# Half pieces of expert weights split three ahead in all sixteen experts of a hybrid decoder block

## The chip, the core and the metric

The kernel runs on one core of a Trainium2 chip. The metric is the device time of one execution in microseconds; where several executions were timed, their median. The engines go by their names in the profile: PE is TensorE (PEld its weight loads), ACT ScalarE, DVE VectorE, POOL GpSimd, SP the engine that here only issues loads and stores.

## The reference

A block over 512 tokens of width 1024: a norm, a pooling mixer and a gated linear recurrence merged by gates, an output projection with a residual, a second norm, and then the part that the change is about, a mixture of 16 experts. Each token goes to two experts of one group. Cut to that part:

```
def hier_moe(h, rg_w, rg_b, re_w, re_b, e_gate, e_up, e_down):
    ...
    for e in range(N_EXP):                      # 16; e_gate, e_up: 1024x512, e_down: 512x1024
        he = jax.nn.silu(xt @ e_gate[e]) * (xt @ e_up[e])
        y = y + comb[:, e:e + 1] * (he @ e_down[e])
```

After it comes a residual and a last norm with a gain. All of it is float32.

## The kernel before

**The stream of weights.** All weights are one list of 124 chunks of 1 MB (512 x 512 numbers for the experts), in the order in which they are used. A chunk is loaded by SP into a raw tile (load_raw, L138, the issue at L143), with at most three loads in flight. Then it is split in two half pieces (split, L150): ScalarE casts a half to float32r, the high part (L151), and VectorE subtracts that from the raw half, the low part (L152). Raw chunks, split half pieces and the transposed rows xt of an expert are tiles of 8 KB per partition in one pool of twenty (b8). weights (L159) is called each time a product is about to read half piece h of chunk c; it first writes out the splits of all half pieces up to 2*c + h + ahead that haven't been written yet, and then the loads.

```
def weights(c, ahead, raw_ahead, h=1):
    while nxt["split"] <= min(2 * c + h + ahead, 2 * len(chunks) - 1):
```

So ahead says how many half pieces beyond the one in use stand in the queues of ScalarE and VectorE by the time its matmuls are written. Each engine works through its queue in order.

**An expert.** Its rows (128 slots) are gathered by GpSimd into xg, transposed by TensorE and split as well (next_x; L718, L504 and L505), and multiplied by the weights as high x high, high x low and low x high (tok_mm, lines L726, L727, L728): six matmuls for a half piece, of which the first needs ScalarE's cast and the second VectorE's subtraction. The order of the chunks is gate of expert e (2 chunks), down of e - 1 (2), up of e (2). The loop at the end writes: first half of gate(e); the hidden state of e - 1 transposed and split (h_parts: L739, then L504 and L505 into ht); second half of gate(e); down(e - 1) in two halves, each evacuated and scaled by ScalarE (L774) and both scattered by GpSimd into x_acc (L743); the next expert's x; up(e), and then the product of the hidden state (L732 on ScalarE, L733 on VectorE). For the last expert the second half of down(14) comes after up(15). Behind that scatter SP reads x_acc back (L879), and the last norm follows.

**What sets how far ahead.** exp_w is the only caller of weights in the experts; its three constants stand before it: three half pieces ahead for chunks below the first gate chunk of expert 12, one from there on, and loads 14 chunks ahead.

```
SPLIT_AHEAD, LATE_AHEAD, RAW_AHEAD = 3, 1, 14
LATE = 12
...
return lambda h: weights(c, SPLIT_AHEAD if c < c_g[LATE][0] else LATE_AHEAD, RAW_AHEAD, h)[h]
```

A scheduler orders the written instructions of each engine by their dependences and by the order of writing, so a few matmuls and casts stand a little beside the written order.

Of the kernel before, what the change touches and what calls it, by code (L numbers as in the profile page):

```python
# [17 lines left out]
P = 128  # L18
S = 512
D = 1024  # L20
KD = D // P
# [15 lines left out]
def tile_hybrid_block(  # L37
# [19 lines left out]
    def b8(shape, dtype, name):  # L57
        return sb.tile(shape, dtype, tag="b8", name=name, bufs=20)

    def s4(shape, dtype, name):  # L60
        return sb.tile(shape, dtype, tag="s4", name=name, bufs=6)

    def s2(shape, dtype, name):
        return sb.tile(shape, dtype, tag="s2", name=name, bufs=5)

    def bank(name):
        return psum.tile([P, 512], F32, tag="ps", name=name)

    def tiny(shape, dtype, name, bufs=2):
        return sb.tile(shape, dtype, tag=name.split("_")[0] + "_t", name=name, bufs=bufs)  # L70

    class Feat:
        """[P, KD, S] in two tiles."""

        def __init__(self, dtype, name):
            self.t = [b8([P, KD // 2, S], dtype, f"{name}{i}") for i in range(2)]
# [15 lines left out]
    tbl = tc.dram_tile([S * NE, 1], I32, name="slot_ids")  # L92
    tblw = tc.dram_tile([S * NE, 1], F32, name="slot_w")

# [1 line left out]
    chunks = []  # L96

    def add(w, r0, rows, c0, n):
# [17 lines left out]
    c_g, c_u, c_d = {}, {}, {}  # L116
# [16 lines left out]
    raws, pairs, loads = {}, {}, {}  # L133
# [4 lines left out]
    def load_raw(upto, after=None):  # L138
        while nxt["raw"] <= min(upto, len(chunks) - 1):
            j = nxt["raw"]  # L140
            ap, kk, n = chunks[j]
            raws[j] = b8([P, kk, n], F32, f"raw{j}")
            loads[j] = SP.dma_start(raws[j], ap).ins  # L143
            if j - IN_FLIGHT in loads:
                tc.add_manual_dep(loads[j], loads[j - IN_FLIGHT].name, SYNC, reason="loads in flight")
            if after is not None:
                tc.add_manual_dep(loads[j], after.name, SYNC, reason="loads yield to it")
            nxt["raw"] += 1
# [5 lines left out]
    def split_half(r, nm):  # L154
        w = b8([P, 2] + list(r.shape[1:]), F32R, f"w{nm}")
        split(r, w[:, 0], w[:, 1])
        return w

    def weights(c, ahead, raw_ahead, h=1):  # L159
        while nxt["split"] <= min(2 * c + h + ahead, 2 * len(chunks) - 1):  # L160
            i, half = divmod(nxt["split"], 2)
            load_raw(i)
            kh = chunks[i][1] // 2
            pairs.setdefault(i, []).append(split_half(raws[i][:, half * kh:(half + 1) * kh], f"{i}_{half}"))
            if half == 1:
                raws.pop(i)
            nxt["split"] += 1
        load_raw((nxt["split"] - 1) // 2 + raw_ahead)
        return pairs[c]

# [1 line left out]
    x_rows = [s4([P, D], F32, f"x_rows{t}") for t in range(NT)]  # L172
    for t in range(NT):
        SP.dma_start(x_rows[t], xr[t * P:(t + 1) * P, :])
# [3 lines left out]
        SP.dma_start(raws[0][:, 4 * h:4 * h + 4], ap0[:, 4 * h:4 * h + 4])  # L178
    nxt["raw"] = 1

# [1 line left out]
    ident = const.tile([P, P], F32, name="ident")  # L182
    make_identity(nc, ident)
    mhalf = const.tile([P, 1], F32, name="mhalf")
# [21 lines left out]
    g1, lam, cb, br, bi, psc, g2f = (par[n] for n in ("g1", "lam", "cb", "br", "bi", "psc", "g2f"))  # L206
    cw = par["cw"].rearrange("p (j c) -> p j c", j=4)

# [1 line left out]
    def rstd_of(src, name):  # L210
        sq = s2([P, D], BF16, f"sq_{name}")
        ssum = tiny([P, 1], F32, f"ssum_{name}", 4)
        ACT.activation(sq, src, AF.Square, accum_out=ssum)
        ms = tiny([P, 1], F32, f"ms_{name}", 4)
        DVE.tensor_scalar(ms, ssum, 1.0 / D, EPS, op0=ALU.mult, op1=ALU.add)
        rs = tiny([P, 1], F32, f"rs_{name}", 4)
        POOL.tensor_tensor(rs, ms, mhalf, op=ALU.pow)
        return rs
# [31 lines left out]
            mm3(ps, w[:, 0], w[:, 1], hi[k], lo[k], k == 0, k == kk - 1)  # L250
        return ps

# [1 line left out]
    sp8 = const.tile([P, KD], F32, name="sp8")  # L254
    nsp8 = const.tile([P, KD], F32, name="nsp8")

    def softplus():
        def small(name):
            return tiny([P, KD], F32, name, 1)

        nlam, mab, ee, den, ss, s2_, acc = (small(n) for n in
                                            ("nlam", "mab", "ee", "den", "ssr", "ssq", "sacc"))
        DVE.tensor_scalar(nlam, lam, -1.0, None, op0=ALU.mult)
        DVE.tensor_tensor(mab, lam, nlam, op=ALU.min)
        ACT.activation(ee, mab, AF.Exp)
        DVE.tensor_scalar(den, ee, 2.0, None, op0=ALU.add)
        DVE.reciprocal(den, den)
        DVE.tensor_tensor(ss, ee, den, op=ALU.mult)
        DVE.tensor_tensor(s2_, ss, ss, op=ALU.mult)
        DVE.tensor_scalar(acc, s2_, 1.0 / 19.0, 1.0 / 17.0, op0=ALU.mult, op1=ALU.add)  # L270
        for k in (15, 13, 11, 9, 7, 5, 3, 1):
            DVE.tensor_tensor(acc, acc, s2_, op=ALU.mult)
            DVE.tensor_scalar(acc, acc, 1.0 / k, None, op0=ALU.add)
        DVE.tensor_tensor(acc, acc, ss, op=ALU.mult)
        DVE.tensor_scalar(nlam, nlam, 0.0, None, op0=ALU.max)
        DVE.scalar_tensor_tensor(acc, acc, 2.0, nlam, op0=ALU.mult, op1=ALU.add)
        DVE.tensor_scalar(sp8, acc, 8.0, None, op0=ALU.mult)
        DVE.tensor_scalar(nsp8, acc, -8.0, None, op0=ALU.mult)

# [1 line left out]
    ra, ix, uu = Lazy(F32, "ra"), Lazy(F32, "ix"), Lazy(F32, "uu")  # L281
    bd = []

# [45 lines left out]
            lru_gates(*pend.pop(0))  # L329
        pend.append(lru_conv(c, ps))  # L330

# [1 line left out]
    icnt = const.tile([P, PAD], F32, name="icnt")  # L333
    for j in range(PAD):
        POOL.memset(icnt[:, j:j + 1], 1.0 / (j + 1))
# [70 lines left out]
                ACT.copy(yh[cc], uu[cc])  # L406
                DVE.tensor_tensor(yl[cc], uu[cc], yh[cc].bitcast(F32), op=ALU.subtract)

# [1 line left out]
    m = Lazy(F32, "m")  # L410
    for j in range(KD):
        wp = weights(c_ga[j // 2], 4, 2)
# [13 lines left out]
        ps = feat_block(wp, (j % 2) * P, KD, xh, xl, f"zgb{j}")  # L426
        ACT.activation(sgb[j], ps, AF.Sigmoid)

# [1 line left out]
    NR = 2 * NG + NE  # L430
    rw = s2([P, KD, NG + NE], F32, "rw")
    POOL.dma_start(rw[:, :, :NG], router_group_w[0].rearrange("(k p) n -> p k n", p=P))
# [51 lines left out]
    rows = const.tile([P, NE], I32, name="rows")  # L484
# [11 lines left out]
            ACT.copy(mt[i][:, 0, j, :], mj)  # L496
            DVE.tensor_tensor(mt[i][:, 1, j, :], mj, mt[i][:, 0, j, :].bitcast(F32), op=ALU.subtract)

# [1 line left out]
    x2s, h2s, xts, xpart, xg = {}, {}, {}, [], []  # L500

    def evac4(tp, hi, lo):
# [4 lines left out]
    def gather(idx, dst, n=S):  # L507
        return POOL.indirect_dma_start(  # L508
            out=dst, out_offset=None, in_=h2d[:n, :],
            in_offset=bass.IndirectOffsetOnAxis(ap=idx, axis=0),  # L510
            bounds_check=n - 1, oob_is_err=False).ins
# [149 lines left out]
    for t in range(NT):  # L661
# [4 lines left out]
        for n in range(2):  # L666
            po = bank(f"po{t}_{n}")
            for kh in range(2):
                w = weights(c_wo[n][kh], 2 if n + kh < 2 else 0, RA[2 * t + n])
                for kk in range(4):  # L670
# [6 lines left out]
                    if kk % 2 == 1:  # L677
# [3 lines left out]
                        if step == 5 and t == NT - 1:  # L681
                            xg.append(s4([P, D], F32, "xg0"))
                            POOL.memset(xg[0], 0.0)
                            first = gather(rows0, xg[0], (NT - 1) * P)
# [59 lines left out]
            out=xd, out_offset=bass.IndirectOffsetOnAxis(ap=idx, axis=0),  # L744
            in_=src, in_offset=None, bounds_check=S - 1, oob_is_err=False, compute_op=ALU.add)

    SPLIT_AHEAD, LATE_AHEAD, RAW_AHEAD = 3, 1, 14
    LATE = 12

    def exp_w(lst, i):  # L750
        c = lst[i]
        return lambda h: weights(c, SPLIT_AHEAD if c < c_g[LATE][0] else LATE_AHEAD, RAW_AHEAD, h)[h]


    def next_x(e):
# [5 lines left out]
    def up(e):  # L761
        pu = bank(f"pu{e}")
        for i in range(2):
            tok_mm(pu, xts[e], 4 * i, exp_w(c_u[e], i), i == 0, i == 1)
            if e + i == 0:
                next_x(1)
        return pu

    def down(e, ht):
        yt = s4([P, D], F32, f"y{e}")  # L770
        for n in range(2):
            py = bank(f"py{e}_{n}")
            tok_mm(py, ht, 0, exp_w(c_d[e], n), True, True)
            ACT.activation(yt[:, n * 512:(n + 1) * 512], py, AF.Copy, scale=wslot[:, e:e + 1])  # L774
            yield
        scatter_add(rows[:, e:e + 1], yt)

    def gate_half(e, pg, i):
        tok_mm(pg, xts[e], 4 * i, exp_w(c_g[e], i), i == 0, i == 1)

# [1 line left out]
    cn = bank("cn")  # L782
    PE.matmul(cn[:, :NE], ones, acum, start=True, stop=True)
    nmf = const.tile([P, 1], F32, name="nmf")
# [27 lines left out]
    back = s2([P, S], F32R, "back")  # L812
# [3 lines left out]
    for i in range(2):  # L816
        weights(c_d[L][i], 0, 0)

# [1 line left out]
    n_max = nc.values_load(nmi[0:1, 0:1], min_val=0, max_val=S)  # L820
    with tc.If(n_max > P):
        emp = s2([P, S * NE // P], I32, "emp")
# [50 lines left out]
                    ACT.activation(og[:, n * 512:(n + 1) * 512], ps, AF.Copy, scale=wsl)  # L873
                scatter_add(sl, og)

# [1 line left out]
    xb = [b8([P, 2, D], F32, f"xb{i}") for i in range(2)]  # L877
    for t in range(NT):
        SP.dma_start(xb[t // 2][:, t % 2, :], xd[t * P:(t + 1) * P, :])  # L879
# [31 lines left out]
    for t, rs in enumerate(frs):  # L911
        for n in range(2):
            c = slice(n * 512, (n + 1) * 512)
# [37 lines left out]
```

## Time and profile before

| what | us |
|---|---|
| median of 3 runs | 697.93 |
| lowest and highest run | 696.56, 698.88 |
| span of the profiled execution | 695.7 |
| TensorE busy in it | 650.9 |
| VectorE busy | 502.5 |
| ScalarE busy | 431.4 |
| GpSimd busy | 79.6 |

The profile is of one execution; its times count from the first instruction. A timeline row has a start, a duration, the engine and line, what is written from what, and in brackets how long the engine sat idle before it and what it waited for. A busy TensorE is not TensorE at its peak: matmuls overlap, so the step from one start to the next tells more than one duration. [...] The experts begin at about 370 us of the span, and the last four take from about 585 to 665 us.

### The profile page before, as it was taken

What the parts mean: (1) busy time and instruction counts of PE and PEld (TensorE: products, weight loads), DVE (VectorE), ACT (ScalarE), POOL (GpSimd) and SP (SyncE); (2) the same over time, 40 slices, a digit from 0 to 9 for tenths busy, and PEclk for the clock granted to TensorE, in tenths of its full rate; (3) what the DMA queues carried; (4) which work ended last, traced back from release to release, by engine and by line L of the source; (5) the groups of instructions that cost most, each with busy time, mean ns of one, the idle gap of its engine ahead of it and who ended that gap; (6) DMA issues with size and microseconds to landing.
All of it is one profiled execution on the core that took longest, in us unless ns stands there. A gap on an engine that the chain in (4) does not pass through costs nothing. (4 is left out here: it accounts for less than half of the span.)

```text
span 695.7 us, 8405 instructions
## 1 busy us (share of the span) xinstructions
PE 650.9 (94%) x3044; PEld 526.8 (76%) x3044; DVE 502.5 (72%) x792; ACT 431.4 (62%) x579; POOL 79.6 (11%) x101
## 2 busy tenths in 40 slices
PE   5999999999999999999959999999999999999970
PEld 4888888788888888887747787777777777777850
DVE  6886699952322227556687898898899888887946
ACT  6599957752213225141244888888888888777913
POOL 3000000000100000000131111111111111101013
PEclk9999999999999999999988999999999999999996
DMA  7920323213217113696584999999999999999134
GB/s 215 345 79 20 127 81 118 95 62 122 65 62 241 53 69 121 235 389 236 198 310 134 334 333 342 341 351 338 331 337 336 361 336 342 335 339 365 53 98 161
DMA packets 88053, 153.23 MB, mean 220 GB/s; under 512 B 7250, under 2 KB 29894, under 8 KB 88009
## 3 DMA queue, kind: packets, MB, share of 16 engines
q1 hardware_dynamic: 81736, 138.98, 57.5%
q0 software_dynamic: 5824, 12.64, 6.8%
q10 hardware_dynamic: 448, 1.05, 0.4%
q8 instruction: 24, 0.39, 0.2%
q14 instruction: 21, 0.16, 0.1%
HBM read 146.67 MB, written 14.16 MB: 231 GB/s over the span
## 5 line engine op out<-in xcount | busy, mean ns | idle before, releaser
L152 DVE TENSOR_TENSOR w<-raw,w 128x1024 fp32r<-128x1024 f32 x248 | 293.6, 1220 | 69.7 <-ACT w L151 67.6
L151 ACT CAST w<-raw 128x1024 fp32r<-128x1024 f32 x248 | 249.7, 1051 | 59.4 <-DVE w L152 14.1
L727 PE MATMUL pu<-w,xt 128*128 128x512 f32 x128 | 51.9, 406 | 2.3 <-DVE w L152 2.3
L726 PE MATMUL pu<-w,xt 128*128 128x512 f32 x128 | 52.2, 408 | 1.8 <-ACT w L151 1.8
L726 PE MATMUL pg<-w,xt 128*128 128x512 f32 x128 | 52.8, 412 | 1.1
L727 PE MATMUL py<-w,ht 128*128 128x512 f32 x128 | 51.6, 403 | 0.0
L728 PE MATMUL py<-w,ht 128*128 128x512 f32 x128 | 50.7, 396 | 0.6 <-DVE ht L505 0.6
L728 PE MATMUL pg<-w,xt 128*128 128x512 f32 x128 | 50.4, 394 | 0.5 <-DVE xt L505 0.5
L728 PE MATMUL pu<-w,xt 128*128 128x512 f32 x128 | 50.7, 396 | 0.0
L727 PE MATMUL pg<-w,xt 128*128 128x512 f32 x128 | 50.3, 393 | 0.3 <-DVE w L152 0.3
L508 POOL DMA_INDIRECT xg<-h_rows,rows x16 | 26.9, 1679 | 197.6 <-PE xtp L718 177.8
L726 PE MATMUL py<-w,ht 128*128 128x512 f32 x128 | 48.8, 395 | 0.8 <-ACT ht L504 0.8
L743 POOL DMA_INDIRECT x_acc<-y,rows x15 | 24.6, 1639 | 62.9 <-ACT y L774 36.4
L727 PEld LDWEIGHTS pu<-w,xt 128*128 128x128 f32 x128 | 24.5, 191 | 8.8 <-DVE w L152 3.2
L726 PEld LDWEIGHTS pg<-w,xt 128*128 128x128 f32 x128 | 24.1, 188 | 9.4 <-ACT w L151 5.3
L726 PEld LDWEIGHTS pu<-w,xt 128*128 128x128 f32 x128 | 24.3, 190 | 7.7 <-ACT w L151 3.1
L726 PEld LDWEIGHTS py<-w,ht 128*128 128x128 f32 x128 | 24.5, 191 | 6.1 <-ACT ht L504 1.0
L505 DVE TENSOR_TENSOR xt<-xtp,xt 128x512 fp32r<-128x512 f32 x30 | 19.4, 686 | 13.4 <-ACT xt L504 13.4
L727 PEld LDWEIGHTS pg<-w,xt 128*128 128x128 f32 x128 | 24.1, 188 | 6.2 <-DVE w L152 0.7
L728 PEld LDWEIGHTS py<-w,ht 128*128 128x128 f32 x128 | 24.4, 191 | 5.7 <-DVE ht L505 1.0
L728 PEld LDWEIGHTS pg<-w,xt 128*128 128x128 f32 x128 | 24.0, 188 | 5.8 <-DVE xt L505 1.1
L728 PEld LDWEIGHTS pu<-w,xt 128*128 128x128 f32 x128 | 24.5, 191 | 4.8
(292 smaller groups left out, 1414.6 us busy)
## 6 DMA issues: line engine op xcount, KB each, us to landing
raw<-in_exp_w_gate_dram SPq DMA_DIRECT2D x32, 1024.0 KB, 8.0
raw<-in_exp_w_up_dram SPq DMA_DIRECT2D x32, 1024.0 KB, 7.9
raw<-in_exp_w_down_dram SPq DMA_DIRECT2D x32, 1024.0 KB, 10.7
raw<-in_w_in_dram SPq DMA_DIRECT2D x17, 1024.0 KB, 7.7
raw<-in_proj_b_dram SPq DMA_DIRECT2D x4, 1024.0 KB, 9.3
raw<-in_w_out_dram SPq DMA_DIRECT2D x4, 1024.0 KB
x_rows<-in_x_dram SPq DMA_DIRECT2D x4, 512.0 KB
xrow<-in_x_dram SPq DMA_DIRECT2D x4, 512.0 KB
```

What stands on the lines that cost most here:

```text
L151: ACT.copy(hi, r)
L152: DVE.tensor_tensor(lo, r, hi.bitcast(F32), op=ALU.subtract)
L505: DVE.tensor_tensor(lo, tv, hi.bitcast(F32), op=ALU.subtract)
L508: return POOL.indirect_dma_start(out=dst, out_offset=None, in_=h2d[:n, :], in_offset=bass.IndirectOffsetOnAxis(ap=idx, axis=0), bounds_che ...
L726: PE.matmul(ps, hi, w[:, 0, k % 2, :], start=first and k == 0, stop=False)
L727: PE.matmul(ps, hi, w[:, 1, k % 2, :], start=False, stop=False)
L728: PE.matmul(ps, lo, w[:, 0, k % 2, :], start=False, stop=last and k == 3)
L743: POOL.indirect_dma_start(out=xd, out_offset=bass.IndirectOffsetOnAxis(ap=idx, axis=0), in_=src, in_offset=None, bounds_check=S - 1, oob_i ...
```

## The change

From expert 12 on the splits are written three half pieces ahead, as for the first twelve, instead of one. The rest of the diff takes comments out, which moves no instruction; the lines behind L747 are one less in the changed kernel.

```
-    SPLIT_AHEAD, LATE_AHEAD, RAW_AHEAD = 3, 1, 14
-    LATE = 12
+    SPLIT_AHEAD, RAW_AHEAD = 3, 14
 
     def exp_w(lst, i):
         c = lst[i]
-        return lambda h: weights(c, SPLIT_AHEAD if c < c_g[LATE][0] else LATE_AHEAD, RAW_AHEAD, h)[h]
+        return lambda h: weights(c, SPLIT_AHEAD, RAW_AHEAD, h)[h]
```

The first place is ScalarE's queue around the start of up(12). raw_4690 and raw_4718 are the two chunks of up(12), raw_4740 the first of gate(13); w_0 and w_1 are the half pieces of a chunk; y is the result of down(11), xt the rows of expert 13. Before:

```order
L774 ACTIVATE y_5036<-py_0_5037,wslot 128x512
L151 CAST w_0_5069<-raw_4690 128x1024
L504 CAST xt_5084<-xtp_0_5085 128x512
L774 ACTIVATE y_5036<-py_1_5059,wslot 128x512
L504 CAST xt_5084<-xtp_1_5092 128x512
L151 CAST w_1_5103<-raw_4690 128x1024
L151 CAST w_0_5112<-raw_4718 128x1024
L151 CAST w_1_5123<-raw_4718 128x1024
```

In the changed kernel:

```order
L773 ACTIVATE y_5044<-py_0_5045,wslot 128x512
L151 CAST w_1_5068<-raw_4690 128x1024
L151 CAST w_0_5077<-raw_4718 128x1024
L773 ACTIVATE y_5044<-py_1_5067,wslot 128x512
L504 CAST xt_5092<-xtp_0_5093 128x512
L504 CAST xt_5092<-xtp_1_5100 128x512
L151 CAST w_1_5111<-raw_4718 128x1024
L151 CAST w_0_5120<-raw_4740 128x1024
```

One cast more stands ahead of the first half of y and two more ahead of the second, and up(12) has three of its four half pieces cast before xt where it had one.

The second place is VectorE's queue after up(13), between the product of the hidden state (silu) and the low part of its transpose (ht, L505). Before:

```order
L733 TENSOR_TENSOR silu_5297<-silu_5297,pu_5258 128x512
L152 TENSOR_TENSOR w_0_5310<-raw_4921,w_0_5310 128x1024
L152 TENSOR_TENSOR w_1_5327<-raw_4921,w_1_5327 128x1024
L152 TENSOR_TENSOR w_0_5336<-raw_4964,w_0_5336 128x1024
L505 TENSOR_TENSOR ht_5319<-htp_5320,ht_5319 128x512
```

In the changed kernel:

```order
L733 TENSOR_TENSOR silu_5303<-silu_5303,pu_5266 128x512
L152 TENSOR_TENSOR w_1_5307<-raw_4921,w_1_5307 128x1024
L152 TENSOR_TENSOR w_0_5316<-raw_4964,w_0_5316 128x1024
L505 TENSOR_TENSOR ht_5325<-htp_5326,ht_5325 128x512
L152 TENSOR_TENSOR w_1_5333<-raw_4964,w_1_5333 128x1024
```

The half pieces between the two are one fewer; the one that left stands ahead of silu.

The third place is the end of ScalarE's queue in the experts: the two halves of y of expert 14, between them what is left to cast of its last down chunk (raw_5231 and raw_5271 before, raw_5217 and raw_5239 in the changed kernel are the two chunks of down(15)). Before:

```order
L774 ACTIVATE y_5489<-py_0_5490,wslot 128x512
L151 CAST w_0_5568<-raw_5231 128x1024
L151 CAST w_1_5581<-raw_5231 128x1024
L151 CAST w_0_5584<-raw_5271 128x1024
L151 CAST w_1_5587<-raw_5271 128x1024
L774 ACTIVATE y_5489<-py_1_5558,wslot 128x512
```

In the changed kernel:

```order
L773 ACTIVATE y_5495<-py_0_5496,wslot 128x512
L732 ACTIVATE silu_5553<-pg_5450 128x512
L151 CAST w_1_5565<-raw_5217 128x1024
L151 CAST w_0_5574<-raw_5239 128x1024
L151 CAST w_1_5587<-raw_5239 128x1024
L773 ACTIVATE y_5495<-py_1_5564,wslot 128x512
```

Three casts stand between the two halves of y where four stood, and the activation of the hidden state of expert 15 (L732) has come between.

## Rows read from the trace of the kernel before

**Rows 1.** The page's first part: busy us (share of the span) xinstructions.
```profile
PE 650.9 (94%) x3044; PEld 526.8 (76%) x3044; DVE 502.5 (72%) x792; ACT 431.4 (62%) x579; POOL 79.6 (11%) x101
```

**Rows 2.** By stage: length, busy PE, PEld, DVE, ACT, POOL (xinstructions), clock, DMA, GB/s.
```profile
580.26:598.50 18.24, 18.13 (x88) 14.56 (x86) 15.89 (x17) 14.13 (x18) 3.45 (x2) 1.00 1.02 354
598.50:618.11 19.61, 18.27 (x87) 14.60 (x86) 16.39 (x16) 15.33 (x18) 2.62 (x2) 1.00 0.99 340
618.11:639.52 21.41, 19.89 (x87) 15.80 (x86) 16.55 (x16) 15.43 (x20) 1.56 (x1) 0.92 1.01 353
639.52:655.52 16.00, 14.81 (x67) 11.67 (x66) 15.25 (x16) 15.82 (x20) 2.15 (x2) 1.00 0.47 150
655.52:663.46 7.94, 7.94 (x37) 6.57 (x35) 7.94 (x10) 4.89 (x6) 0.00 (x0) 1.00 0.01 3
```

**Rows 3.** TensorE's timeline: start us, us, engine, line, operation, [idle before, releaser].
```profile
592.70 0.39 PE L728 MATMUL py<-w,ht 128*128 128x512 f32 x1
...
600.72 0.51 PE L726 MATMUL pu<-w,xt 128*128 128x512 f32 x1 [0.59 <-ACT w L151]
601.98 0.50 PE L727 MATMUL pu<-w,xt 128*128 128x512 f32 x1 [0.75 <-DVE w L152]
...
620.50 0.49 PE L726 MATMUL pu<-w,xt 128*128 128x512 f32 x1 [0.75 <-ACT w L151]
621.76 0.50 PE L727 MATMUL pu<-w,xt 128*128 128x512 f32 x1 [0.77 <-DVE w L152]
...
640.77 0.40 PE L728 MATMUL pu<-w,xt 128*128 128x512 f32 x1
641.58 0.49 PE L726 MATMUL pu<-w,xt 128*128 128x512 f32 x1 [0.42 <-ACT w L151]
642.84 0.50 PE L727 MATMUL pu<-w,xt 128*128 128x512 f32 x1 [0.77 <-DVE w L152]
643.18 0.40 PE L728 MATMUL pu<-w,xt 128*128 128x512 f32 x1
...
660.96 0.39 PE L726 MATMUL py<-w,ht 128*128 128x512 f32 x1
...
663.46 0.39 PE L728 MATMUL py<-w,ht 128*128 128x512 f32 x1
```

**Rows 4.** ScalarE's timeline, the same columns; x2, x4: so many in a row.
```profile
578.28 2.01 ACT L151 CAST w<-raw 128x1024 fp32r<-128x1024 f32 x2
...
581.93 1.08 ACT L504 CAST xt<-xtp 128x512 fp32r<-128x512 f32 x2 [0.92 <-PE pu L728]
...
599.15 0.58 ACT L504 CAST xt<-xtp 128x512 fp32r<-128x512 f32 x1
599.61 2.00 ACT L151 CAST w<-raw 128x1024 fp32r<-128x1024 f32 x2
...
656.52 3.89 ACT L151 CAST w<-raw 128x1024 fp32r<-128x1024 f32 x4
663.88 0.69 ACT L774 ACTIVATE y<-py,wslot 128x512 f32<-128x512 f32 x1 [3.47 <-PE py L728]
```

**Rows 5.** One stretch behind the waits of expert 13; columns as in rows 2.
```profile
622.79:626.67 3.88, 3.88 (x12) 3.03 (x11) 3.56 (x4) 2.81 (x4) 0.00 (x0) 0.56 1.05 340
```

**Rows 6.** GpSimd's timeline: the scatter of expert 10 and that of expert 14.
```profile
582.94 1.59 POOL L743 DMA_INDIRECT x_acc<-y,rows  x1 [0.30 <-issue]
...
664.85 2.35 POOL L743 DMA_INDIRECT x_acc<-y,rows  x1 [22.80 <-DVE w L152]
```

**Rows 7.** The chain that ended last, in order of time: start us, us, what.
```profile
674.63 6.98 DMA xb<-x_acc
```

**Rows 8.** VectorE's timeline: L505 of expert 11, and six subtractions in a row.
```profile
591.48 0.68 DVE L505 TENSOR_TENSOR ht<-htp,ht 128x512 fp32r<-128x512 f32 x1
...
651.85 6.89 DVE L152 TENSOR_TENSOR w<-raw,w 128x1024 fp32r<-128x1024 f32 x6
```

**Rows 9.** SP's queue: the load that waits for the last weights.
```profile
646.36 0.35 SPq L881 DMA_DIRECT2D gfb<-in_norm_f_g_dram  x1
```

## The prediction

> **What bounds the kernel now.** The page's first part [rows 1] has TensorE busy for 650.9 of 695.7 us, so time can be won only where TensorE waits or runs at the lower clock. The change touches the last four experts alone, so I cut the span at the start of each expert's "up" product (its first matmul into pu) and read busy time by stage [rows 2]. The reader is to see three things there. A stage of the first twelve experts takes 18.24 us (expert 11, from 580.26), with TensorE busy for 18.13 of it. The stages of experts 12 and 13 take 19.61 and 21.41 us for the same work. DMA stands at 1.01 of its engines and 353 GB/s in the second of them and falls to 0.47 in the next: loads run flat out until they are over.
>
> Then TensorE's timeline [rows 3]. In up(12), up(13) and up(14) the seventh matmul, the first on the second half piece of the weights, waits 0.42 to 0.75 us for ScalarE's cast (L151), and the eighth, the first to read the low part, another 0.75 to 0.77 us for VectorE's subtraction (L152). The reason stands in ScalarE's timeline [rows 4]. In expert 10 two casts, from 578.28, lie ahead of the last evacuation of the "down" product, and the two copies of the next x (L504) follow at 581.93. In expert 12 the second copy comes at 599.15 and the cast that TensorE waits for only behind it, at 599.61.
>
> [...]
>
> The end hangs on TensorE: the second half of down(14) starts its last matmul at 663.46 [rows 3], ScalarE scales it at 663.88 [rows 4], GpSimd scatters it at 664.85 [rows 6], and the last read-back of the scattered rows lands 6.98 us after 674.63 [rows 7]. From 663.46 on the rest is a chain of transfers and the final norm, some 32 us, that the change doesn't touch.
>
> **The change, part by part.** No instruction is added or taken away. What moves is the place of the half pieces' cast and subtraction in the queues of ScalarE and VectorE, two half pieces (one chunk) earlier. The queues of SP and GpSimd stand as before.
>
> *Waits removed.* A matmul takes 0.227 us (eleven steps from 660.96 to 663.46 [rows 3]), so a half piece of six is 1.36 us of TensorE, and two pieces more ahead ask for a split 2.7 us sooner. In expert 14 the three steps from 640.77 to 643.18 take 2.41 us and should take 0.68 [rows 3]: the pair of waits costs 1.73 us. 2.7 us of lead covers that. What each stage gets back:
> - expert 12: 19.61 - 18.24 = 1.37 us [rows 2]. The order then is that of the first twelve, so the pace is theirs.
> - expert 13: 21.41 - 18.24 = 3.17 us [rows 2]. The clock is in it: 3.88 us at 0.56 [rows 5] is 2.17 us of work at full clock, 1.7 us lost.
> - expert 14: 1.73 us by its own steps, as its stage has another make-up.
>
> Together 6.27 us. All of it lies on TensorE ahead of 663.46, so it moves the end by as much, if nothing else comes late. What is late next:
>
> *VectorE.* From 639.52 to 663.46 it is busy for 15.25 + 7.94 = 23.2 of 23.9 us [rows 2]. With 1.73 us of waits gone the stretch has 22.2 us. But two half pieces less fall in it: six subtractions in a row take 6.89 us [rows 8], 1.15 each, so 20.9 us of work remain, a margin of 1.3 us. In the stages of 12 and 13 it is busy for at most 16.55 us, under 18.24. The near thing is its low part of the hidden state (L505): for expert 11 it starts at 591.48, takes 0.68 [rows 8] and is first read at 592.70 [rows 3], 0.5 us in hand. In experts 13 and 14 the order is not quite that of the first twelve, and half a microsecond may come back in each. I bound this by 0 and 1.0 us in all and take 0.2, near to zero, since no more subtractions stand ahead of L505 there than before.
>
> *Loads.* The load of the final gain, issued at 646.36 [rows 9], waits for the last weights to land; their casts are the last two of the four from 656.52 [rows 4], the first of them at about 658.5: 12 us in hand. Casts come 6.1 us earlier with TensorE and 2.7 by the change, which leaves some 3 us, so this costs nothing; without that cover each microsecond of lateness is one of TensorE. Two half pieces more hold two more tiles of the twenty in their pool and free one raw tile sooner; the loads are paced by the DMA engines at 1.01, not by tiles, so I take nothing for that.
>
> *The scatter at the end.* It took 2.35 us where an earlier one took 1.59 [rows 6]. VectorE was subtracting beside it; by my count it still will be. If it is done by then, up to 0.76 us falls off the end: I take 0 and keep 0.76 for the range.
>
> Sum on the profiled execution: 695.7 - 6.27 + 0.2 = 689.6 us. The median of the runs is 697.93, 2.2 us above that execution's span; I carry this over: 691.8 us.
>
> **Rivals.**
> 1. *The clock doesn't fall in most runs.* It falls behind one of three like pairs of waits [rows 2, 3], so in the timed runs it may stay up, and then 1.7 us of the 6.27 can't be won: 697.9 - 4.4 = 693.5 us. For it: the runs spread over 2.3 us. Against: the profiled execution, fall and all, is no longer than they are. [...]
> 2. *VectorE becomes the bound.* It works first come, first served; if the margin of 1.3 us is eaten and waits come back at "down" of experts 12, 13 and 14, at about 1 us each, 6.1 - 3 = 3.1 us are won, 694.8 us. For it: 23.2 of 23.9 us busy. Against: the count above.
> 3. *The loads set the pace.* Then a wait taken from TensorE comes back as a wait for weights, and nothing is won: 697.9 us. For it: DMA at 1.01 up to the stage of expert 13. Against: the 12 us between the last landing and its casts. [...]
> 4. *It doesn't do what it says.* If the late casts wait for tiles that TensorE still reads, they move in the queue but not in time: 697.9 us. Against: expert 11 runs in 18.24 us with as many tiles and the same order.
> 5. *Slower.* VectorE comes to L505 in down(12), down(13) and down(14) only after two subtractions more. Each is then late by 2 x 1.15 - 0.5 = 1.8 us, and after such a wait the clock falls as in [rows 5], 1.7 us more: 3 x 3.5 - 6.3 = 4.2 us lost, 702.1 us. It costs from 0.5 us of delay on, and turns the sign where each of the three costs over 2.1 us. Against: the new order has two subtractions between the product of the hidden state (L733) and L505 for expert 13, where there were three.
>
> **How the numbers follow.** Forecast 0.66, clock 0.18, VectorE 0.06, loads 0.03, no effect 0.03, slower 0.04. A measurement of this kernel can tell about 0.3% from no change, 2.1 us. Faster by more: forecast, clock and VectorE, 0.90; within it: loads and no effect, 0.06; slower 0.04. The range: at the low end the forecast less 0.76 us for the scatter and about 1 us, half the runs' spread, 690.0; at the high end rival 1 with 1.0 us for L505 and half a microsecond of spread, 695.0, which takes in rival 2.
>
> **What would show it.** Right: the stages of experts 12 and 13 at 18.2 to 18.5 us, that of 14 at 14.3; no wait for weights above 0.3 us at the seventh and eighth matmul of up(12) to up(14); the clock at 1.00 from 600 to 660; the last matmul of down(14) near 657.4; the last weights landed near 646 as before; some 32 us from there to the end. Wrong: new waits of TensorE at "down" on L505 or L152, a cast that waits for a load, or an end that doesn't move with TensorE.

## The result, and the profile after

The changed kernel takes 691.12 us (median of 4 runs, 689.7 to 694.0) beside 698.4 us of the kernel before on the same chip: ratio 0.990, 95% interval 0.9869 to 0.993, 4.9 to 9.1 us. A second comparison, told below, gave 0.993 (0.9902 to 0.9958). Forecast were 691.8 us and faster.

The profiled execution of the changed kernel has a span of 689.2 us. Line numbers behind L747 are one less than before. Its busy times, as in [rows 1]:

```profile
PE 648.4 (94%) x3044; PEld 525.1 (76%) x3044; DVE 502.1 (73%) x792; ACT 430.9 (63%) x579; POOL 80.4 (12%) x101
```

The same stages as in [rows 2], from one start of "up" to the next, then the stretch of all of them (length, busy PE, PEld, DVE, ACT, POOL, the granted clock as a share of full speed, DMA, GB/s):

```profile
580.78:599.01 18.23, 18.11 (x87) 14.54 (x86) 16.45 (x17) 15.42 (x19) 3.45 (x2) 1.00 0.98 336
599.01:617.25 18.24, 18.12 (x88) 14.56 (x86) 16.46 (x17) 15.43 (x19) 3.46 (x2) 1.00 0.95 327
617.25:635.45 18.20, 18.08 (x87) 14.58 (x85) 17.24 (x18) 15.34 (x21) 1.89 (x1) 1.00 1.02 346
635.45:649.62 14.17, 14.17 (x68) 11.74 (x66) 13.84 (x15) 14.17 (x18) 2.15 (x2) 1.00 0.81 274
649.62:657.55 7.93, 7.93 (x36) 6.57 (x35) 7.93 (x10) 4.56 (x6) 0.00 (x0) 1.00 0.17 70
600.00:660.00 60.00, 58.57 (x270) 47.27 (x269) 56.60 (x58) 50.05 (x60) 8.08 (x6) 1.00 0.80 274
```

Experts 12 and 13 now take what expert 11 takes. Their 19.61, 21.41 and the 16.00 of expert 14 [rows 2] have become 18.24, 18.20 and 14.17: 6.41 us. The seventh and eighth matmul of up(14), which waited 0.42 and 0.77 us [rows 3], now follow at one step, and the only wait that the matmul rows show from 600 to 664 us stands behind the last expert, in down(15):

```profile
636.91 0.39 PE L726 MATMUL pu<-w,xt 128*128 128x512 f32 x1
637.14 0.39 PE L727 MATMUL pu<-w,xt 128*128 128x512 f32 x1
...
659.76 0.50 PE L726 MATMUL py<-w,ht 128*128 128x512 f32 x1 [1.05 <-ACT ht L504]
```

One kind of wait for a weight is left behind the first expert, and it stands only on the rows of TensorE's weight loads (PEld): in the stages of experts 2 to 13 the load for the first matmul of the next gate, which stands inside "up", waits 0.54 us for ScalarE's cast. The kernel before had it in experts 2 to 11. Its row is shown under "What is late next?".

The end, in the views of [rows 4] and [rows 6 to 9]: ScalarE's last casts of weights, the last scatter on GpSimd, the last read-back in the chain, VectorE's L505 of expert 14, and SP's load behind the last weights.

```profile
651.22 2.95 ACT L151 CAST w<-raw 128x1024 fp32r<-128x1024 f32 x3
...
658.94 1.92 POOL L743 DMA_INDIRECT x_acc<-y,rows  x1 [20.96 <-ACTq L820]
...
668.35 6.83 DMA xb<-x_acc
...
646.05 0.68 DVE L505 TENSOR_TENSOR ht<-htp,ht 128x512 fp32r<-128x512 f32 x1
...
649.32 0.35 SPq L880 DMA_DIRECT2D gfb<-in_norm_f_g_dram  x1
```

The scatter is 0.43 us shorter than before (2.35 us [rows 6]), and the last weights land 3 us later than in [rows 9]. From the last matmul of down(14), at 657.55, to the end it is 31.7 us; it was 32.2. The end follows the scatter: SP's first read-back is issued 6.0 us after the scatter's end before (667.20 and 673.24 us) and 6.1 us after it in the changed kernel (660.86 and 666.92 us).

### The profile page after: what moved, and what is told of

It is laid out like the page before. It is cut to its first block, busy times and chain, and to the rows that moved or that the text cites. A ratio compares the mean times of both kernels' runs of the same rounds, so it can differ in the third digit from the quotient of the medians.

```text
span 689.2 us, 8411 instructions
## 1 busy us (share of the span) xinstructions
PE 648.4 (94%) x3044; PEld 525.1 (76%) x3044; DVE 502.1 (73%) x792; ACT 430.9 (63%) x579; POOL 80.4 (12%) x101
## 3 DMA queue, kind: packets, MB, share of 16 engines
HBM read 146.67 MB, written 14.16 MB: 233 GB/s over the span
## 5 line engine op out<-in xcount | busy, mean ns | idle before, releaser
L726 PE MATMUL pu<-w,xt 128*128 128x512 f32 x128 | 51.2, 400 | 0.0
L727 PE MATMUL pu<-w,xt 128*128 128x512 f32 x128 | 51.1, 399 | 0.0
L727 PE MATMUL py<-w,ht 128*128 128x512 f32 x128 | 50.9, 398 | 0.0
L728 PE MATMUL pu<-w,xt 128*128 128x512 f32 x128 | 50.1, 391 | 0.0
L728 PE MATMUL py<-w,ht 128*128 128x512 f32 x128 | 49.9, 390 | 0.0
L726 PE MATMUL py<-w,ht 128*128 128x512 f32 x128 | 48.1, 391 | 1.0 <-ACT ht L504 1.0
L726 PEld LDWEIGHTS py<-w,ht 128*128 128x128 f32 x128 | 24.0, 188 | 6.2 <-ACT ht L504 1.3
L728 PEld LDWEIGHTS py<-w,ht 128*128 128x128 f32 x128 | 24.1, 188 | 5.0 <-DVE ht L505 0.4
L727 PEld LDWEIGHTS py<-w,ht 128*128 128x128 f32 x128 | 24.1, 188 | 4.5
```

The source lines that it names most:

```text
L726: PE.matmul(ps, hi, w[:, 0, k % 2, :], start=first and k == 0, stop=False)
L727: PE.matmul(ps, hi, w[:, 1, k % 2, :], start=False, stop=False)
L728: PE.matmul(ps, lo, w[:, 0, k % 2, :], start=False, stop=last and k == 3)
```

## The experiments

**Theory**: TensorE waits in up(12) to up(14) because one half piece of lead is too little; three remove the waits, and the time follows TensorE. **Rivals**: the waits come from the place near the end (loads running out) and not from the lead; the clock's fall of expert 13 [rows 5] is not in most runs; the loads or VectorE take over as the bound.

### How much lead, and for which expert

The first kernel leaves only the last two experts at one piece; the second gives the last four two pieces; the third gives, on top of one, a lead to the second half piece of "up" alone, in experts 12 to 14.

```diff
-    LATE = 12
+    LATE = 14
```

> Splits run three half pieces ahead up to the chunks of down(12) and up(13), one ahead from gate(14) on. Theory (the waits come from too little lead in front of up, stage by stage): the stages of experts 12 and 13 take 18.2 us each as in the changed kernel, the waits of 0.4 and 0.8 us come back at the seventh and eighth matmul of up(14) alone, whose stage takes 16.0 us; 1.4 + 3.2 = 4.6 us less than the kernel before, 1.8 more than the changed one; if the clock falls behind the waits of up(14), 1.7 us more than that. Rival (VectorE's total work in the last stretch sets the end): nothing or little is won, since the two half pieces are again in the last stretch.

```diff
-    SPLIT_AHEAD, LATE_AHEAD, RAW_AHEAD = 3, 1, 14
+    SPLIT_AHEAD, LATE_AHEAD, RAW_AHEAD = 3, 2, 14
```

> From gate(12) on two half pieces ahead instead of one. The second half piece of up now stands ahead of the copies of the next x in ScalarE's queue, the third behind them. Theory of lead: the pair of waits cost 1.73 us at one ahead, one piece more of lead is worth 1.36 us, so 0.4 to 0.5 us of waits stay in each of up(12) to up(14), now at the third half piece (thirteenth matmul), and without the fall of the clock the kernel gets 6.4 - 1.4 = 5 us faster than before. Rival theory of place (it only matters that the second half piece stands ahead of the copies of x): no wait stays, 6.4 us.

```diff
+            if e >= LATE:
+                weights(c_u[e][0], 0, RAW_AHEAD)
```

(put ahead of next_x(e + 1); it writes the splits up to the second half of the first chunk of "up")

> One ahead from gate(12) on as in the kernel before, but for experts 12 and 13 (and 14, whose next x is written at the same place) the split of the second half piece of up is written just ahead of the next x; nothing else moves. Theory of lead: as with two ahead, 0.4 to 0.5 us of waits stay in each up, at the third half piece; stages of 18.7 us; about 5 us faster than before. Theory of place: stages of 18.2 us, 6.4 us faster. If other half pieces (gate, down) also needed their lead, less than 5 us.

Measured: 694.01 us (ratio 0.9937, 0.991 to 0.9965), 694.28 us (0.9947, 0.9924 to 0.9969) and 693.03 us (0.9926, 0.9894 to 0.9959). The first, by stage for experts 12 to 14, and the waits of its up(14):

```profile
601.05:619.28 18.23, 18.11 (x87) 14.55 (x86) 16.45 (x17) 15.42 (x19) 3.45 (x2) 1.00 0.99 320
619.28:637.49 18.21, 18.09 (x87) 14.59 (x86) 15.41 (x16) 13.58 (x19) 1.88 (x1) 1.00 1.01 347
637.49:653.43 15.94, 14.74 (x67) 11.66 (x66) 15.19 (x16) 15.82 (x20) 2.14 (x2) 1.00 0.77 256
...
639.55 0.50 PE L726 MATMUL pu<-w,xt 128*128 128x512 f32 x1 [0.44 <-ACT w L151]
640.81 0.50 PE L727 MATMUL pu<-w,xt 128*128 128x512 f32 x1 [0.76 <-DVE w L152]
```

The two waits of "up" stand where the lead is one and nowhere else. The second kernel, the stages and the only two waits for weights on their matmul rows:

```profile
599.99:619.05 19.06, 18.31 (x88) 14.49 (x86) 16.49 (x17) 15.21 (x18) 2.88 (x2) 1.00 0.98 320
619.05:637.80 18.75, 17.99 (x88) 14.66 (x86) 17.26 (x17) 15.49 (x20) 1.56 (x1) 1.00 1.00 354
637.80:652.40 14.60, 14.50 (x68) 11.67 (x66) 13.85 (x15) 14.60 (x18) 2.14 (x2) 1.00 0.78 267
...
603.97 0.50 PE L727 MATMUL pu<-w,xt 128*128 128x512 f32 x1 [0.75 <-DVE w L152]
623.02 0.50 PE L727 MATMUL pu<-w,xt 128*128 128x512 f32 x1 [0.76 <-DVE w L152]
```

Two pieces remove the wait for the cast and leave one for a subtraction, at the fourteenth matmul, in the third half piece, where the theory of lead had it: 0.82, 0.55 and 0.43 us over the changed kernel's stages, 1.8 of the 4.8 to 6.4 us. In up(14) that wait stands on the weight-load row alone (0.52 us, at 641.12). For the first two that is more than the 0.4 to 0.5 us expected, and the gain, 3.8 us (2.2 to 5.3), is below the 5 us expected but not clear of it. The third kernel shows the same (19.10, 18.77 and 14.63 us, one wait of 0.76 us each in up(12) and up(13)): what the second piece of lead buys, it buys in "up" alone; gate and down gain nothing from it.

### Is it the lead or the place?

One half piece of lead in all sixteen experts:

```diff
-    SPLIT_AHEAD, LATE_AHEAD, RAW_AHEAD = 3, 1, 14
+    SPLIT_AHEAD, LATE_AHEAD, RAW_AHEAD = 1, 1, 14
```

> One half piece of lead in all sixteen experts, not in the last four alone. Theory (the lead of one makes the waits at the seventh and eighth matmul of up, wherever it stands): stages 1 to 11 grow from 18.24 to 19.6 to 19.8 us, each with a wait of about 0.59 us on ScalarE's cast and one of about 0.75 us on VectorE's subtraction; 11 times 1.4 to 1.6 us is 15 to 18 us, 713 to 716 us, and more if the clock falls after the waits: each fall adds 1.6 us (21.41 against 19.80 us for stage 13), and by the two looks at the kernel before it comes in one of six such stages, so some 3 us more. Rival (the waits of the last four come from the end of the loads, not from the lead): stages 1 to 11 stay at 18.24 us and the time at 698 us.

Measured: 712.91 us (ratio 1.0226, 1.0193 to 1.0259). Two of its stages, of experts 1 and 2, and the waits at the start of the second:

```profile
398.20:417.93 19.73, 18.32 (x87) 14.61 (x86) 16.62 (x16) 15.45 (x19) 3.50 (x2) 1.00 0.91 311
417.93:439.38 21.45, 19.94 (x87) 15.73 (x86) 16.62 (x16) 15.73 (x19) 2.61 (x2) 0.92 1.00 329
...
420.32 0.50 PE L726 MATMUL pu<-w,xt 128*128 128x512 f32 x1 [0.76 <-ACT w L151]
421.58 0.50 PE L727 MATMUL pu<-w,xt 128*128 128x512 f32 x1 [0.76 <-DVE w L152]
```

The second has the clock's fall behind its waits (0.92 over the stage). The stages of experts 3 to 13 take 19.6 us. The place has nothing to do with it: they pay 1.4 us each for a lead of one, far from the end as near it.

### Is the clock's fall in every run?

The kernel before, profiled twice more, and the changed kernel once more, all unchanged.

> The kernel before, profiled once more. The pairs of waits of up(12), up(13) and up(14) come again with 1.2 to 1.5 us of idle time each. If the fall of the clock belongs to the waits of expert 13, the stage of 13 takes 21.4 us again; if it comes by chance behind any of the three pairs or none, one of the three stages is longer by 1.7 us or none is, and the stage of 13 takes 19.6.

> The kernel before, a third profile of it. Both theories: waits of about 0.59 and 0.75 us in up(12) and up(13), 0.42 and 0.75 us in up(14), stage 12 at 19.6 us, 14 at 16.0 us. Theory (the clock's fall comes in some runs only): stage 13 at 19.8 us with the clock at 1.00, or at 21.4 us with a fall; a fall after up(12) or up(14) would be as likely. Rival (the fall belongs to expert 13, and the second look was the exception): 21.4 us.

> The changed kernel once more, in more rounds. Theory (the gain is the waits of up(12) to up(14), and the clock's fall in expert 13 comes in some runs only): stages 12 and 13 at 18.2 us, 14 at 14.2 us, no wait above 0.3 us at a matmul of up, clock 1.00 from 600 to 660 us, and a median of 690 to 692 us, some 7 us below the kernel before. Rival (the three or four runs so far were lucky, and only the 4.8 us of stages that the second look at the kernel before gives up is there): 693 to 694 us.

The stages of experts 12 and 13 in the first repeat, then those waits of expert 13 in the second that in [rows 3] preceded the fall:

```profile
599.28:618.94 19.66, 18.31 (x88) 14.61 (x85) 16.38 (x16) 15.33 (x18) 2.62 (x2) 1.00 0.99 331
618.94:638.74 19.80, 18.29 (x88) 14.65 (x86) 16.37 (x16) 15.23 (x20) 1.56 (x1) 1.00 1.04 354
...
622.50 0.49 PE L726 MATMUL pu<-w,xt 128*128 128x512 f32 x1 [0.75 <-ACT w L151]
623.75 0.50 PE L727 MATMUL pu<-w,xt 128*128 128x512 f32 x1 [0.77 <-DVE w L152]
```

Both repeats have the same waits to within 0.02 us, 19.80 us in expert 13 and the clock at 1.00: the fall is in one profile of three, and worth 1.6 us there (21.41 - 19.80). That one profile has a second fall, behind the waits of down(15) for ht (0.76 us for ScalarE's part, 0.60 us for VectorE's), which the repeats don't have after nearly the same waits (columns as in [rows 2]):

```profile
667.33:670.74 3.41, 3.41 (x10) 2.65 (x9) 0.00 (x0) 0.00 (x0) 0.00 (x0) 0.50 0.51 72
```

It cost the end nothing, as the end waited for the scatter and not for down(15). The changed kernel repeated at 691.52 us beside 696.36 (11 runs), ratio 0.993 (0.9902 to 0.9958), with stages of 18.27, 18.25 and 14.16 us. Without the fall the three stages give 19.66 + 19.80 + 15.96 - 50.61 = 4.8 us.

A kernel without any lead was for the clock alone:

```diff
-    SPLIT_AHEAD, RAW_AHEAD = 3, 14
+    SPLIT_AHEAD, RAW_AHEAD = 0, 14
```

> No lead at all: each half piece is split where it is used, in all experts. It is for the clock. So far two falls of the clock to 0.50 were seen, each after two waits of 0.75 to 0.77 us with one piece of work between them, in two of the four stages that had such a pair; none in the nineteen stages whose first wait was shorter (0.42 to 0.66 us), and none after a single wait of 0.76 us. Theory (the fall comes after idle stretches of that size close together, by chance): with three or more waits of 0.75 us or more in every stage, the clock falls in most of the fifteen stages, each such stage 1.6 us or more longer, and the mean granted clock in the experts is below 0.95. Rival (the two falls have nothing to do with the waits' lengths): no more than two falls. The time itself: each stage 2 to 5 us longer than with a lead of one, 740 to 780 us.

Measured: 742.21 us in its one run, and eight falls to 0.50 in fifteen stages. TensorE's waits in two neighbouring stages, and these stages with their clock:

```profile
447.69 0.79 PE L726 MATMUL pu<-w,xt 128*128 128x512 f32 x1 [2.14 <-ACT w L151]
448.95 0.80 PE L727 MATMUL pu<-w,xt 128*128 128x512 f32 x1 [0.46 <-DVE w L152]
470.80 0.50 PE L727 MATMUL pu<-w,xt 128*128 128x512 f32 x1 [0.76 <-DVE w L152]
472.81 0.51 PE L727 MATMUL pu<-w,xt 128*128 128x512 f32 x1 [0.34 <-DVE w L152]
...
447.69:469.54 21.85, 21.36 (x84) 16.50 (x84) 16.05 (x16) 14.34 (x17) 1.06 (x1) 0.85 0.90 306
469.54:491.38 21.84, 18.60 (x84) 14.65 (x84) 17.23 (x18) 16.63 (x21) 5.68 (x4) 1.00 0.95 316
```

There are two kinds of stage: in nine TensorE waits 1.67 to 2.14 us for the cast before it waits for the subtraction, and the clock falls in eight; in six the waits are 0.76 and 0.35 us, and it never falls. Five of the eight falls begin before the second wait is over, and the one shown at 447.53 us, before the first is (it ends at 447.69, and the matmul then takes 0.79 us where others behind a wait take 0.50): there one long wait came ahead of the fall, and not two. With the waits of "up" in the other profiles: two falls in four stages with a pair of 0.75 to 0.77 us, none in twenty whose first wait was 0.42 to 0.66 us, none after a single 0.76 in four. Behind the pair of down(15), 0.76 and then 0.59 us or more, the clock fell in three of seven profiles. My words there, "three or more waits in every stage", were wrong (two in each), and the mean clock of the experts is 0.95, at the bound given. Longer first waits go with more falls; why one of two equal pairs is followed by a fall and the other isn't stays open.

At the kernel's start, too, the three profiles of the kernel before differ: from 15 to 19 us one has the clock at 0.57 and the other two at 1.00. The fall in expert 13 differs from run to run in the same way, in the middle of the kernel.

### What is late next?

More lead than the change gives, four pieces everywhere:

```diff
-    SPLIT_AHEAD, RAW_AHEAD = 3, 14
+    SPLIT_AHEAD, RAW_AHEAD = 4, 14
```

> Three to four in all sixteen experts. By the order of the instructions the first matmul of the gate, which in the changed kernel stands inside the last pieces of up in every expert (0.51 us instead of 0.23 us to the next matmul at 585.48, and 0.34 us after it), then stands behind up's last matmul. Theory (TensorE is the bound, and only such changes of place and the weights' lead cost it time): a stage of 18.24 us goes to 17.8 to 17.9 us, twelve of them, and the time to 686 to 688 us. Rival (no gain: the extra time at that place is that of a switch between two banks and comes wherever the gate begins): 18.2 us and 690.5 to 692 us. Rival (the fourth pair of buffers for split weights is taken from the loads, and they become late): stages of 18.5 us or more with waits on w, above 693 us.

Measured: 690.22 us (0.9904, 0.988 to 0.9928), little less than the changed kernel and above the 686 to 688 us expected. TensorE in the changed kernel, where the gate's first matmul stands inside "up", with its weight load, in expert 11, and then the same place in expert 1; then, of four pieces everywhere, the stages of experts 12 and 14, ScalarE at the end of the second, and TensorE behind it:

```profile
584.97 0.39 PE L726 MATMUL pu<-w,xt 128*128 128x512 f32 x1
585.47 0.19 PEld L726 LDWEIGHTS pg<-w,xt 128*128 128x128 f32 x1 [0.54 <-ACT w L151]
585.48 0.50 PE L726 MATMUL pg<-w,xt 128*128 128x512 f32 x1
585.81 0.47 PE L727 MATMUL pu<-w,xt 128*128 128x512 f32 x1
...
403.16 0.39 PE L726 MATMUL pu<-w,xt 128*128 128x512 f32 x1
403.38 0.39 PE L726 MATMUL pg<-w,xt 128*128 128x512 f32 x1
403.61 0.39 PE L727 MATMUL pu<-w,xt 128*128 128x512 f32 x1
```

```profile
596.52:614.37 17.85, 17.85 (x88) 14.62 (x86) 16.45 (x17) 15.14 (x20) 3.44 (x2) 1.00 1.00 344
632.44:648.27 15.83, 14.76 (x67) 11.60 (x66) 12.93 (x15) 12.42 (x16) 2.15 (x2) 1.00 0.97 337
...
642.62 1.99 ACT L151 CAST w<-raw 128x1024 fp32r<-128x1024 f32 x2 [2.63 <-DMA raw<-in_exp_w_up_dram]
644.52 0.58 ACT L504 CAST ht<-htp 128x512 fp32r<-128x512 f32 x1
...
645.14 0.50 PE L726 MATMUL py<-w,ht 128*128 128x512 f32 x1 [1.07 <-ACT ht L504]
```

The size came out, the reason didn't. A stage takes 17.85 us instead of 18.24, and TensorE idles nowhere in it. But the place inside "up" costs nothing by itself: in expert 1 of the changed kernel the gate's first matmul stands there too, the steps before and behind it are 0.22 and 0.23 us, and that stage takes 17.70 us. Where the steps are 0.51 and 0.33 us, the load of this matmul's weights waits 0.54 us for ScalarE's cast. So it is the mechanism of the whole change once more, a cast that comes late with three pieces of lead and not with four; no weight load of the gate waits in these stages with four pieces. Eleven stages (experts 2 to 12) gained it, not the twelve that I counted: 4.3 us, of which the span kept 1.2 (689.2 to 688.0). Expert 0 lost 1.2 us (21.1 against 19.9), the scatter took its 2.35 us again, and expert 14 lost 1.66 us: ScalarE waited 2.63 us for a load, and the cast of ht, for which TensorE stood idle, was queued behind. ScalarE kept to the order of its queue: TensorE had finished the transpose of ht at 641.55 us, but the cast of it began at 644.52, behind the two that the load held up. The load is that of the second chunk of up(15). In the changed kernel it landed at 638.98 us and its cast began at 645.42, 6.4 us in hand. With four pieces ScalarE was ready for it 5.4 us sooner, at 639.99, and it landed 3.6 us later, at 642.54, 11.1 us after its issue instead of 8.0. Why the transfer took longer is not shown.

Two ways out, three pieces of lead again in expert 0 and from expert 13, or one load more in flight with four pieces:

```diff
-    SPLIT_AHEAD, RAW_AHEAD = 3, 14
+    SPLIT_AHEAD, MID_AHEAD, RAW_AHEAD = 3, 4, 14
...
-        return lambda h: weights(c, SPLIT_AHEAD, RAW_AHEAD, h)[h]
+        ahead = MID_AHEAD if c_g[1][0] <= c < c_g[13][0] else SPLIT_AHEAD
+        return lambda h: weights(c, ahead, RAW_AHEAD, h)[h]
```

> Four half pieces of lead from expert 1 to 12, three in expert 0 and from expert 13. With four everywhere, stages 1 to 12 went to 17.84 us, and stage 0 grew by 1.2, stage 13 to 18.08 and stage 14 to 15.83 us. Theory (stage 14 was lost on ScalarE, where the cast of a piece whose load lands at 642.5 us stands ahead of the cast of ht, for which TensorE waits): with three pieces there, that cast stands behind ht's, stage 14 goes back to 14.2 to 14.6 us, stage 0 to 19.9 to 20.3 us, and the time to 687 to 688.5 us, 2 to 3 below four everywhere. Rival (the last loads land near 650 us whatever the order, so that earlier experts only wait for them elsewhere): another wait of 1 to 2 us on w in up(14), down(14) or in the tail, and 690 us.

```diff
-    IN_FLIGHT = 3
+    IN_FLIGHT = 4
...
-    SPLIT_AHEAD, RAW_AHEAD = 3, 14
+    SPLIT_AHEAD, RAW_AHEAD = 4, 14
```

> Four half pieces of lead in all experts, and four loads of weights in flight instead of three. Theory (the transfers are the bound, a mean of 0.98 to 1.00 of the DMA engines busy at 330 to 350 GB/s in the stages of the experts): the rate stays at 330 to 350 GB/s, the last load lands at 648 to 651 us again, stage 14 stays at 15.5 to 16 us, and the time at 690 us. Rival (the limit is the wait for a load three back): the rate goes to 360 GB/s or more, the last load lands 3 us or more earlier, stage 14 goes to 14.2 us, and the time to 687 to 688.5 us.

Measured: 686.55 us (0.9853, 0.983 to 0.9877) and 687.45 us (0.9876, 0.9852 to 0.990). The first beats both kernels, by a little more than expected. Its stages of experts 13 and 14 and ScalarE there; then the last stage of the second, and its ScalarE:

```profile
613.57:631.27 17.70, 17.70 (x88) 14.75 (x86) 17.32 (x18) 15.41 (x21) 2.02 (x1) 1.00 0.99 335
631.27:645.43 14.16, 14.16 (x67) 11.75 (x66) 13.92 (x15) 13.53 (x17) 2.16 (x2) 1.00 1.05 354
...
640.75 0.59 ACT L504 CAST ht<-htp 128x512 fp32r<-128x512 f32 x1
641.22 2.01 ACT L151 CAST w<-raw 128x1024 fp32r<-128x1024 f32 x2
643.86 2.00 ACT L151 CAST w<-raw 128x1024 fp32r<-128x1024 f32 x2 [0.63 <-DMA raw<-in_exp_w_down_dram]
```

```profile
632.12:646.31 14.19, 14.19 (x68) 11.76 (x66) 14.05 (x16) 12.34 (x16) 2.14 (x2) 1.00 0.83 285
...
643.28 2.00 ACT L151 CAST w<-raw 128x1024 fp32r<-128x1024 f32 x2 [1.25 <-DMA raw<-in_exp_w_down_dram]
```

With three pieces, the cast that depends on a load stands behind ht's, and expert 14 is back at 14.16 us; the loads are hardly earlier (that one lands at 641.16 instead of 642.54 us, and ScalarE still waits 0.63 us for the next, to no harm). With four loads in flight neither expectation held whole: the rate stayed (0.97 to 1.04 of the DMA engines busy in experts 2 to 13, a mean of 344 GB/s beside 339 with three in flight), yet expert 14 went to 14.19 us. The load in question was issued at 626.87 and landed at 638.26 us, 4.5 and 4.3 us before the 631.41 and 642.54 of three in flight. So a fourth load in flight hardly raised the rate, but it started the transfers earlier, and a few us are enough here.

## Why the prediction was right, point by point

- **TensorE bounds, and its waits move the end one for one**: right, but not as closely as the totals look. 6.41 us left the stages and 6.5 us the span (695.7 to 689.2); between these two profiles the stage of expert 11 began 0.52 us later (580.26, 580.78), so the last matmul of down(14) came 5.91 us earlier, and the other half microsecond came off the end. The three profiles of the kernel before differ by 2 us in that start alone (580.26 to 582.27).
- **Expert 12, 1.37 us**: 1.37 (19.61 to 18.24). The pace of the first twelve, which the prediction took over as it is, itself holds 0.39 us of a wait: that of the gate's weight load. **Expert 14, 1.73 us**: 1.83; the steps of the two waits alone gave a little too little.
- **Expert 13, 3.17 us**: 3.21 between these two profiles, but mis-sized for the runs: 1.6 of it is the clock's fall, which two of three profiles don't have. The three pairs of waits were taken as alike, but their first waits are 0.59, 0.75 and 0.42 us [rows 3], and the experiments have no fall behind a pair at "up" whose first wait is 0.42 to 0.66 us. Rival 1's mechanism is thus what most of the profiles show, and at 0.18 its chance was too low. Its time, 693.5, was not met, for two reasons: 697.93 was the median of only three runs (49 runs of all comparisons, on several chips, give 697.06), and the end gained 0.4 us that no case counted. From 697.06, with 4.8 us of waits, 0.43 of the scatter and a third of 1.6 us for the clock, it is 691.3 us; the ten runs of the changed kernel have a median of 691.1. That one fall in three holds for the runs is not shown: it rests on three profiles. Without any clock it is 691.8 us, the forecast itself. So the time can't tell the forecast from rival 1's mechanism, and neither can the two comparisons on one chip each, 7.3 and 4.8 us; that the forecast's number was met is in part luck.
- **The scatter**: taken at 0, with 0.76 us kept for the range; it gave 0.43. As it starts, VectorE is in a subtraction in both kernels, which ran on for 0.90 us before (to 665.75) and for 0.47 us after (to 659.41); the scatter's excess over 1.59 us is 0.76 and 0.33. With four loads in flight the subtraction ended 0.08 us after the start, and the scatter took 1.58 us.
- **L505, 0.2 us taken**: nothing came back. It starts at 628.39 for expert 13 and at 646.05 for expert 14, as shown above, and no matmul of these stretches waits for it. **VectorE**: no wait, but thinner than I worked out. In 22.10 us it is busy for 13.84 + 7.93 = 21.77; I had 20.9 of 22.2. Two subtractions less were taken from this stretch, and only 1.4 us left it: the stage of expert 13 rose from 16.55 to 17.24.
- **Loads, "some 3 us in hand"**: 2.9 us, from the load in the SP row, which waits for the last landing and follows at 649.32, to the last two casts, which begin at 652.17. The size is right by two errors that cancel. The landing was not near 646; it was at 649.4 and 650.3 us in the two repeats of the kernel before, too, so [rows 9] was an early one. And the last two casts came 6.2 us earlier (from 658.40), not 6.1 + 2.7: only one cast less stands between the first half of y and them, and the activation of expert 15 has come between (the third place under "The change"). That the cover was real is shown by four pieces everywhere, where it was gone: these casts begin at 650.44, as the last weights land (SP's load follows at 650.49). Rival 3 misses the changed kernel by these 2.9 us, and by 6.4 us at the load of up(15); four pieces everywhere, where a cast waited for that load and TensorE for the cast behind, are such a case in one stage.
- **The offset**: 2.2 us were carried over from the span to the median; time less span is 1.7 us in the typical run of either kernel. The rest was the three runs.
- **Rivals 4 and 5** have nothing for them: the casts moved in time, and no new wait came at "down" of experts 12 to 14.

The signs named in advance came: 18.2, 18.2 and 14.2 us, no wait at the seventh and eighth matmul of up(12) to up(14), clock 1.00 from 600 to 660, last matmul of down(14) at 657.55 (forecast 657.4), 31.7 us behind it. Only the landing of the last weights missed.

## What to carry to other kernels

Where an engine prepares operands for another through one queue, look for the consumer whose preparation stands behind a burst of other work (here "up", behind the next x) and give that one the lead first: the second half piece of "up" alone gave 2.9 of the 4.8 us (55.42 to 52.50 us in the three stages). Then read the weight-load rows too: a wait that showed on no matmul row cost 0.39 us in each of eleven stages. More lead moves a cast closer to its load (that of up(15)'s second chunk had 6.4 us in hand with three pieces and waited 2.63 us with four), and what was queued behind the waiting cast came late too (ht, for 1.07 us of TensorE), so end the extra lead before the loads run out. And take a loss of clock seen in one profile as a chance until a second profile shows it.

## What was not expected of the hardware

- The granted clock fell to 0.50 of full speed for 3.4 us after TensorE had been idle only twice for 0.75 to 0.77 us with one step of work between, in two of four such stages; after 0.42 to 0.66 us and 0.76 us, in none of twenty; after 0.76 us and 0.59 us or more in down(15), in three of seven. Where the first wait was 1.67 to 2.14 us, it fell in eight stages of nine, twice for 6.8 us, and once before that first wait was over.
- A wait for an operand can stand on TensorE's weight-load row alone: 0.54 us there left no wait on the matmul rows, only steps of 0.51 and 0.33 us instead of 0.23, and 0.39 us more in the stage. A matmul of another product inside a run of accumulating ones cost nothing where its weights were ready (expert 1 of the changed kernel: steps of 0.22 and 0.23 us).
- The scatter on GpSimd took longer than 1.59 us by 0.76 us where VectorE was still subtracting for 0.90 us after its start, by 0.33 us where for 0.47 us, and by nothing where for 0.08 us.
